# Two sets of small products taken over the whole TensorE array, and the written-out order of a layer made from other costs and waits

## The chip, the core and the metric

The kernel runs on one core of one Trainium2 chip. The metric is the device time of one execution in microseconds (us), from the first to the last instruction with what lies around them. A core has a matrix engine (TensorE, PE in the profile, with its weight loads as PEld), a vector engine (VectorE, DVE), a scalar engine (ScalarE, ACT), GpSimd (POOL) and SyncE (SP), which here only issues loads. Each engine works off its own list of instructions in the order in which the program wrote them; an instruction that waits for another engine holds up everything behind it in its own list.

## The reference

One layer of a hybrid decoder is computed for 256 tokens of a new sequence and for 8 running sequences ("samples") of 8 tokens each, 320 tokens in all. All arithmetic is float32:

```python
h = rms_norm(x, norm_g)
p = einsum('nld,dp->nlp', h, w_in)              # 2048 -> 12416 columns
# branch A, 16 heads of 64: RWKV-7 state, one step per token
sa = einsum('nhvk,nhk->nhv', s, kk_t)
s  = s * w_t - sa (kk_t * a_t)^T + v_t k_t^T;   y_t = s r_t
# branch B, 8 heads of 128: gated linear recurrence
S_t = diag(g_t) S_{t-1} + k_t v_t^T;            o_t = S_t^T q_t
merged = sigmoid(ga) * (y_a @ proj_a) + sigmoid(gb) * (y_b @ proj_b)
y = rms_norm(x + merged @ w_out, final_norm_g)
```

The states after the last token of every sequence are outputs too; the samples start from states that are loaded.

## The kernel before

**Stages.** A start stage normalizes and transposes x. Then comes the long stage this text is about, here the *recorded stage*: 64 column tiles of `w_in` that the heads need, and four gate tiles, each multiplied with the 320 tokens, and in between them all the recurrence work of eight head groups (one group is two heads of branch A and one head of branch B). After it the remaining gate tiles, `proj_a`, `proj_b` and `w_out` follow.

**Stream.** Float32 weights and activations are each split into a rounded high part and a remainder, and a product is three matmuls: high by high, high by low, low by high. A column tile is 16 times three matmuls of 128x128 weights with 320 columns into the tile `mps`. The text calls these matmuls the *stream*. The weights come in blocks of 512 KB (`raw`, by SyncE), ScalarE copies the high part (`whi`), VectorE subtracts for the remainder (`wlo`); each has three buffers.

**Head work.** `rwkv` (L706) and `hgrn` (L1071) hold the recurrences in a form for matmuls. For branch B a 64-token chunk is worked by levels: `level` (L1118) makes scaled keys and queries `kq` for block sizes 8 to 128, `products` (L1139) multiplies them, and `keep` (L1145) copies the wanted triangles of the result out of PSUM (`b`) into `att` by a mask. `products` runs one matmul for each 64-token chunk: 64 columns of weights, 64 columns streamed, and neighbouring chunks go to the upper and the lower half of the PSUM partitions, so that two such matmuls use two halves of the array's columns. In branch A `samples` (L980) multiplies the samples' states `s0t` with `arz` in the same way, eight matmuls for a group. These float32 matmuls are not split by the program; the profile shows each of them as two passes (two records).

**Order.** The recorded stage isn't issued as it is written. `Recorder` (L69) takes every call down as an `Op` with a cost in ns by engine and shape (`add`), finds who must wait for whom (`link`, L141), and then plays the engines against the clock (`order`, L175). At each step `choose` (L191) takes the engine that can begin first and picks an operation on it: on PE a small matmul in the whole-array shape as soon as it is ready, small matmuls of other shapes (`part`) together, those of `hgrn` after a wait of up to 6000 ns (`WAIT`), and else the next matmul of the stream; on VectorE and ScalarE the weight splits first when the stream comes within 4500 ns of them, else what has the longest chain behind it. A small matmul on whose result an operation depends counts as late by `LAT` and by a margin of 250 ns (`MARGIN`). The result is one fixed list for each engine (L1340); on the chip, semaphores keep the data right, and a list that was made from wrong times shows as waits.

**What the costs know.** In the plan of before each engine runs by itself: VectorE's and GpSimd's operations never delay each other. A load that overwrites a buffer which a store still reads (the state `s0`, loaded at L718 and L1073 and stored at the end of the group before, all issued by GpSimd) may in the plan follow that store at once.

Of the kernel before, what the change touches and what calls it, by code (L numbers as in the profile page):

```python
# [12 lines left out]
AF = mybir.ActivationFunctionType  # L13
# [35 lines left out]
class Op:  # L49
    __slots__ = ("eng", "fn", "args", "kw", "cost", "lat", "uses", "mode", "passes", "cols", "stream",  # L50
                 "succ", "npred", "ready", "rank", "block", "margin", "wait", "n")
# [17 lines left out]
class Recorder:  # L69
    APART, MARGIN, WAIT = 10, 250, 6000  # L70
# [14 lines left out]
    def add(self, eng, name, fn, args, kw):  # L85
        o = Op()
        o.eng, o.fn, o.args, o.kw, o.n = eng, fn, args, kw, len(self.ops)
        aps = [x for x in (*args, *kw.values()) if hasattr(x, "start_partition")]
        out = aps[0]
        free = 1  # L90
        for d in out.shape[1:]:
            free *= d
        o.uses = []
        for j, x in enumerate(aps):
            t_ = x.tensor
            if "DRam" in type(t_).__name__:
# [5 lines left out]
        o.lat = self.LAT[eng]  # L102
        o.mode = None
# [71 lines left out]
    def order(self):  # L175
# [8 lines left out]
        mode, done, left = (128, 128), [], len(self.ops)  # L184
        bigs = [o for o in self.ops if o.eng == "PE" and o.stream]
# [5 lines left out]
        def choose(e):  # L191
# [3 lines left out]
            t_ = max(now, min(o.ready for o in q))  # L195
# [17 lines left out]
            can = [o for o in q if o.ready <= t_ + 30]  # L213
# [8 lines left out]
        while left:  # L222
            t_, o = min((choose(e) for e in ready if ready[e]), key=lambda x: x[0])
# [5 lines left out]
            if o.eng == "PE":  # L229
# [5 lines left out]
                if o.stream:  # L235
                    gone += 1
            free[o.eng] = end = start + cost
# [9 lines left out]
def hybrid_step(ctx, tc, x_prompt, x_sample, state_rwkv, state_hgrn, state_shift, norm_g, w_in,  # L247
# [384 lines left out]
    def ring(pool, tag, shape, bufs, dt, size, clear=False):  # L632
# [12 lines left out]
        if len(shape) == 2:  # L645
# [5 lines left out]
             "w1": 320, "w2": 320, "w3": 320, "ks": 128, "ket": 256}  # L651


    CLEAR = {"uB", "uE", "ys", "rhs", "rhs2", "k3", "vm"}
# [51 lines left out]
    def rwkv(p, r, k, vp, za):  # L706
# [273 lines left out]
        def samples():  # L980
            ps = aps("psr")
            for sp in range(4):
                for h in range(2):
                    T.matmul(ps[HS[h], 32 * sp:32 * sp + 32], s0t[:, sp, 64 * h:64 * h + 64],
                             arz[:, sp, :, h].rearrange("p b x i -> p b (x i)"), start=True, stop=True)

            sr0, sr1 = at("sr0", (128, 2, 64)), at("sr1", (128, 64))
            p4 = ps[:, :128].rearrange("p (s x i) -> p x s i", x=2, i=8)
            V.tensor_copy(sr0.rearrange("p h (s i) -> p h s i", i=8), p4[:, 0:1].to_broadcast([128, 2, 8, 8]))
            S.copy(sr1.rearrange("p (s i) -> p s i", i=8), p4[:, 1])  # L990
# [80 lines left out]
    def hgrn(hd, q, k, v, zb):  # L1071
# [37 lines left out]
        k0 = bt("k0", tag="w1")  # L1109
        S.activation(k0, x, AF.Exp, scale=-1.0)  # L1110
        V.tensor_mul(q0, q0, q)
        V.tensor_mul(k0, k0, k)
# [5 lines left out]
        def level(sz, tag):  # L1118
            half = lambda t_: t_[:, :NP_].rearrange("p (b two s) -> p b two s", two=2, s=sz)
            kq = bt("kq", (128, NP_), tag=tag)  # L1120
            if sz == 32:
# [23 lines left out]
        def keep(ps, o_, n):  # L1145
            for c_ in range(2):
                sl = HS[c_]
                V.copy_predicated(att[sl, :NP_].rearrange("p (j c t) -> p j c t", c=2, t=64)[:, :, c_],
                                  mu8[sl, None, n].to_broadcast([64, 2, 64]),
                                  ps[sl, o_:o_ + 128].rearrange("p (j t) -> p j t", t=64))  # L1150
# [3 lines left out]
        products(ps, 0, k0, q0, 5)  # L1154
        products(ps, 256, kq8, kq8)
        keep(ps, 0, 0)
        V.copy_predicated(att[0:64, NP_:], mu8[0:64, 0], ps[0:64, 128:192])
# [19 lines left out]
        ps = bps("pke")  # L1177
        T.transpose(ps[0:64, :128], es[:, 1], ident)
        k3 = bt("k3", (128, 2, 128), dt=F32R)
# [8 lines left out]
        T.matmul(ps[:, 256:320], vt[0:64, 2], att[0:64, NP_:], start=True, stop=True)  # L1188
# [18 lines left out]
        for j in range(2):  # L1207
            T.matmul(ps[HS[j], 128:192], kq32[:, 64 * j:64 * j + 64], kq32[:, 128 + 64 * j:192 + 64 * j],
                     start=True, stop=True)
        for j in range(2):  # L1210
            T.matmul(ps[HS[j], 192:256], kq64[:, 128 * j:128 * j + 64], kq64[:, 128 * j + 64:128 * j + 128],
                     start=True, stop=True)
        keep(ps, 0, 2)
        for j in range(2):
            for b in range(2):
                V.tensor_copy(att[64 * b:64 * b + 32, 128 * j + 64 * b + 32:128 * j + 64 * b + 64],
                              ps[64 * j + 32 * b:64 * j + 32 * b + 32, 128 + 32 * b:160 + 32 * b])
            V.tensor_copy(att[0:64, 128 * j + 64:128 * j + 128], ps[HS[j], 192:256])
# [289 lines left out]
```

## Time and profile before

| what | value |
|---|---|
| median of 3 runs | 1195.76 us (1194.38 to 1198.14) |
| profiled execution, its own time | 1195.58 us |
| its span, first to last instruction | 1193.8 us |
| busy, share of the span: PE, PEld, DVE, ACT, POOL | 96%, 92%, 66%, 56%, 22% |
| the chain that ended last: PE, DVE, ACT | 82%, 8%, 3% |
| recorded stage, first to last stream matmul of its list (L1341) | 35.4 to 755.5 us |

A line of the profile names the source line, the engine, the operation, the tile written and the tiles read (`out<-in`), shapes and counts. All operations of the recorded stage have one line, L1341, and many tiles share a ring: `a` is any PSUM tile of `rwkv`, `b` any of `hgrn`, `w` the rings w1 to w3 of `hgrn` (levels, keys, queries), `s` the states. "Idle before" is the time in which the engine did nothing, with what ended it. PE's matmuls overlap in the pipeline, so a matmul's duration is longer than its distance to the next one; costs on PE are read here as distances between starts.

### The profile page before, as it was taken

To read this page: it belongs to the slowest core of one execution; us is meant where nothing else is said; L and a number is where in the kernel's file an instruction comes from. 1 tells how busy PE (TensorE), PEld (TensorE's weight loads), DVE (VectorE), ACT (ScalarE), POOL (GpSimd) and SP (SyncE) were. 2 spreads that over 40 slices of the span, in tenths; PEclk is the share of its full clock that TensorE was granted. 3 is DMA by queue.
4 is the path that set the end of the run, shared out by engine and by line. 5 is a ranking of instruction groups with operands and counts; after the bars stand their busy time and mean duration, and the time that the engine had idled before them with its cause. 6 is when DMAs were issued, how large, how long until landed. Compare 5 with 4: busy or idle time off the path is not lost.

```text
span 1193.8 us, 21136 instructions
## 1 busy us (share of the span) xinstructions
PE 1151.3 (96%) x7976; PEld 1096.4 (92%) x7976; DVE 790.3 (66%) x1618; ACT 666.3 (56%) x1463; POOL 258.5 (22%) x493
## 2 busy tenths in 40 slices
PE   5999999999999999999998999999999999999997
PEld 4898998998998998999998998999999999998875
DVE  7678878778868968869777877644344444435552
ACT  6566765766666667557666666544444444434431
POOL 7642333243323323413413312000000000000000
PEclk9899999999999999999999999999999999999999
DMA  6442543543534534524534435555555555575542
GB/s 181 127 136 81 160 121 89 148 122 91 148 106 128 144 85 113 146 80 127 139 110 113 131 83 137 151 150 151 146 155 147 154 145 156 144 254 163 169 135 88
DMA packets 251424, 159.72 MB, mean 134 GB/s; under 512 B 5609, under 2 KB 237338, under 8 KB 250682
## 3 DMA queue, kind: packets, MB, share of 16 engines
q1 hardware_dynamic: 246106, 140.68, 41.3%
q0 software_dynamic: 5216, 17.68, 5.4%
q8 instruction: 63, 1.03, 0.4%
q14 instruction: 39, 0.32, 0.1%
HBM read 148.53 MB, written 9.81 MB: 133 GB/s over the span
## 4 chain that ended last, share of the span: by engine, by line
PE 82%; DVE 8%; ACT 3%; DMA 2%; POOL 2%; issue 2%; DVEq 0%; SPq 0%; ACTq 0%; POOLq 0%
PE mps L1341 36%; PE a L1341 10%; PE mps L313 6%; PE mps L312 6%; PE mps L311 6%; PE b L1341 3%; DMA raw<-in_w_out_dram 2%; PE po L1423 2%; PE po L1421 2%; PE po L1422 2%; PE ppb L313 2%; PE ppa L313 2%; PE ppb L312 2%; PE ppa L312 2%; PE ppb L311 2%
## 5 line engine op out<-in xcount | busy, mean ns | idle before, releaser
L1341 PE MATMUL mps<-hlo,whi 128*128 128x320 f32 x1088 | 347.1, 319 | 0.0
L1341 PE MATMUL mps<-hhi,wlo 128*128 128x320 f32 x1088 | 346.4, 318 | 0.4 <-DVE wlo L1341 0.4
L1341 PE MATMUL mps<-hhi,whi 128*128 128x320 f32 x1088 | 344.7, 317 | 1.9 <-ACT whi L1341 1.9
L1341 PEld LDWEIGHTS mps<-hhi,whi 128*128 128x128 f32 x1088 | 206.3, 190 | 3.7 <-ACT whi L1341 2.2
L1341 PEld LDWEIGHTS mps<-hhi,wlo 128*128 128x128 f32 x1088 | 206.4, 190 | 2.4 <-DVE wlo L1341 0.8
L1341 PEld LDWEIGHTS mps<-hlo,whi 128*128 128x128 f32 x1088 | 206.5, 190 | 1.2 <-issue 0.6
L302 DVE TENSOR_TENSOR wlo<-raw,whi 128x1024 fp32r<-128x1024 f32 x88 | 107.7, 1225 | 125.0 <-ACT whi L301 124.8
L1341 DVE TENSOR_TENSOR wlo<-raw,whi 128x1024 fp32r<-128x1024 f32 x134 | 168.9, 1261 | 20.2 <-ACT whi L1341 19.0
L301 ACT CAST whi<-raw 128x1024 fp32r<-128x1024 f32 x88 | 92.1, 1048 | 161.1 <-PE mps L312 107.2
L1341 ACT CAST whi<-raw 128x1024 fp32r<-128x1024 f32 x134 | 140.3, 1048 | 73.5 <-PE mps L1341 70.6
L311 PE MATMUL mps<-hhi,whi 128*128 128x320 f32 x464 | 145.0, 312 | 0.0
L312 PE MATMUL mps<-hlo,whi 128*128 128x320 f32 x464 | 144.7, 312 | 0.0
L313 PE MATMUL mps<-hhi,wlo 128*128 128x320 f32 x464 | 144.7, 312 | 0.0
L313 PEld LDWEIGHTS mps<-hhi,wlo 128*128 128x128 f32 x464 | 88.3, 190 | 0.0
L312 PEld LDWEIGHTS mps<-hlo,whi 128*128 128x128 f32 x464 | 88.2, 190 | 0.0
L311 PEld LDWEIGHTS mps<-hhi,whi 128*128 128x128 f32 x464 | 88.1, 190 | 0.0
L1414 DVE TENSOR_TENSOR wlo<-raw,whi 128x1024 fp32r<-128x1024 f32 x32 | 39.0, 1224 | 44.5 <-ACT whi L1413 44.4
L1396 POOL DMA_DIRECT2D xb<-in_x_sample_dram x1 | 0.5, 546 | 312.9 <-PE mps L313 312.9
L1413 ACT CAST whi<-raw 128x1024 fp32r<-128x1024 f32 x32 | 33.5, 1050 | 54.3 <-PE po L1426 23.3
L1423 PE MATMUL po<-wlo,mhi 128*128 128x512 f32 x128 | 50.4, 394 | 0.9 <-DVE wlo L1414 0.9
L1421 PE MATMUL po<-whi,mhi 128*128 128x512 f32 x128 | 50.2, 392 | 0.7 <-DVE gbt L1381 0.7
L1422 PE MATMUL po<-whi,mlo 128*128 128x512 f32 x128 | 50.0, 391 | 0.0
(418 smaller groups left out, 2356.0 us busy)
## 6 DMA issues: line engine op xcount, KB each, us to landing
raw<-in_w_in_dram SPq DMA_DIRECT2D x194, 512.0 KB
raw<-in_w_out_dram SPq DMA_DIRECT2D x32, 512.0 KB
raw<-in_proj_a_dram SPq DMA_DIRECT2D x16, 512.0 KB
raw<-in_proj_b_dram SPq DMA_DIRECT2D x16, 512.0 KB
s<-in_state_hgrn_dram POOLq DMA_DIRECT2D x8, 512.0 KB, 5.5
out_dram<-s POOLq DMA_DIRECT2D x8, 512.0 KB, 4.6
s<-in_state_rwkv_dram POOLq DMA_DIRECT2D x8, 256.0 KB, 4.0
out_dram<-s POOLq DMA_DIRECT2D x8, 256.0 KB, 3.3
```

Of the source, the lines that this page charges most:

```text
L301: S.copy(hi[:, ks], raw[:, ks])
L302: sub.tensor_sub(lo[:, ks], raw[:, ks], hi[:, ks].bitcast(F32))
L311: T.matmul(dst, hi[:, q, :], xhi[:, k, :], start=(k == 0), stop=False)
L312: T.matmul(dst, hi[:, q, :], xlo[:, k, :], start=False, stop=False)
L313: T.matmul(dst, lo[:, q, :], xhi[:, k, :], start=False, stop=(k == nk - 1))
L1341: o.fn(*o.args, **o.kw)
L1396: G.dma_start(yx[j], src)
L1413: S.copy(hi, raw)
L1414: V.tensor_sub(lo, raw, hi.bitcast(F32))
L1421: T.matmul(pt, h, hi, start=first, stop=False)
L1422: T.matmul(pt, l, hi, start=False, stop=False)
L1423: T.matmul(pt, h, lo, start=False, stop=end)
```

## The change

On TensorE: `products` multiplies 128 tokens with 128 tokens in one matmul over the whole array and `keep` picks the two 64-token diagonal blocks out of the larger result; levels 32 and 64 become one matmul each; the samples' part of the first level gets a matmul of its own, later, beside the transposition of `es`; the samples' `vt` by `att` runs over all 128 rows, with the unused rows cleared once; the state products become four matmuls in place of eight, and `sr0` and `sr1` are copied out in two halves each.

In the plan: every operation has a mark `port` if it needs the port that VectorE and GpSimd are taken to share, and `hold` if it keeps the other engine from it (two inputs that are not in PSUM, or a VectorE copy or `tensor_scalar` all in SBUF). An operation with `port` begins no earlier than the other engine's hold ends, less 130 ns. A load waits in the plan for the landing of a store that reads its buffer (4500 ns). The fixed costs of VectorE, ScalarE and GpSimd operations are changed.

The core of the diff (the bookkeeping around it, and shapes that only follow, are left out):

```diff
+        two = sum("PSUM" not in str(x.space) for x in aps[1:] if tuple(x.shape[1:]) != (1,)) > 1
+        o.hold = two and eng in "VG"
+        o.port = two and eng == "V" or eng == "G" and "dma" not in name
...
-            o.cost = (free / 2 if two else free) / 0.96 + (215 if two else 157)
+            o.cost = (free / 2 if two else free) / 0.96 + (150 if two else 157)
+            if two:
+                o.hold = o.port = True
+            if any(tuple(x.shape[1:]) == (1,) and free > 1 for x in aps[1:]):
+                o.cost += 55
...
-            o.cost = 190 + free / 1.2
+            o.cost = (150 if name == "copy" else 200) + free / 1.2
+            if name == "copy" and not o.uses[1][5]:
+                o.cost += 40
...
-            o.cost = 950 if "dma" in name else 250 + free * (0.35 if name == "memset" else 1.75)
+            o.cost = 950 if "dma" in name else 95 + free * 0.88 if name == "memset" else 200 + free * 1.66
...
-                            pred.setdefault(u[3].n, (u[3], psum and u[3].eng != "PE"))
+                            pred.setdefault(u[3].n, (u[3], psum and u[3].eng != "PE" or u[3].dma))
...
+            if e in port:
+                held = port["G" if e == "V" else "V"] - self.OVER
+                if e == "V" and held > now and port["G"] == free["G"]:
+
+                    held += min((o.cost for o in ready["G"] if o.hold and o.ready <= free["G"] - 40), default=0.0)
+                at_ = {o: max(now, o.ready, held if o.port else 0.0) for o in q}
+                t_ = min(at_.values())
...
-            for h in range(2):
-                    T.matmul(ps[HS[h], 32 * sp:32 * sp + 32], s0t[:, sp, 64 * h:64 * h + 64],
-                             arz[:, sp, :, h].rearrange("p b x i -> p b (x i)"), start=True, stop=True)
+                T.matmul(ps[:, 64 * sp:64 * sp + 64], s0t[:, sp], arz[:, sp].rearrange("p b h x i -> p (b h x i)"),
+                         start=True, stop=True)
...
-        def products(ps, o_, kq, q_, n=4):
-            for c_ in range(n):
-                tk_ = slice(64 * c_, 64 * c_ + 64)
-                T.matmul(ps[HS[c_ % 2], o_ + 64 * (c_ // 2):o_ + 64 * (c_ // 2) + 64], kq[:, tk_], q_[:, tk_],
-                         start=True, stop=True)
+        def products(ps, o_, kq, q_):
+            for j in range(2):
+                tk_ = slice(128 * j, 128 * j + 128)
+                T.matmul(ps[:, o_ + 128 * j:o_ + 128 * j + 128], kq[:, tk_], q_[:, tk_], start=True, stop=True)
...
-        products(ps, 0, k0, q0, 5)
+        products(ps, 0, k0, q0)
...
         ps = bps("pke")
+        T.matmul(ps[:, 128:192], k0[:, NP_:], q0[:, NP_:], start=True, stop=True)
...
-        T.matmul(ps[:, 256:320], vt[0:64, 2], att[0:64, NP_:], start=True, stop=True)
+        T.matmul(ps[:, 256:320], vt[:, 2], att[:, NP_:], start=True, stop=True)
...
-        for j in range(2):
-            T.matmul(ps[HS[j], 128:192], kq32[:, 64 * j:64 * j + 64], kq32[:, 128 + 64 * j:192 + 64 * j],
-                     start=True, stop=True)
-        for j in range(2):
-            T.matmul(ps[HS[j], 192:256], kq64[:, 128 * j:128 * j + 64], kq64[:, 128 * j + 64:128 * j + 128],
-                     start=True, stop=True)
+        T.matmul(ps[:, 256:384], kq32[:, 0:128], kq32[:, 128:256], start=True, stop=True)
+        T.matmul(ps[:, 384:512], kq64[:, 0:128], kq64[:, 128:256], start=True, stop=True)
```

More of the change, by code (lines that the diff above doesn't have):

```diff
@@ L50 @@
     __slots__ = ("eng", "fn", "args", "kw", "cost", "lat", "uses", "mode", "passes", "cols", "stream",
-                 "succ", "npred", "ready", "rank", "block", "margin", "wait", "n")
+                 "succ", "npred", "ready", "rank", "block", "margin", "wait", "port", "hold", "dma", "n")
 def span_of(ap):
@@ L102, in add @@
         o.lat = self.LAT[eng]
+        o.dma = "dma" in name
         o.mode = None
@@ L130, in add @@
         elif eng == "S":
-            o.cost = 190 + free / 1.2
+            o.cost = (150 if name == "copy" else 200) + free / 1.2
+            if name == "copy" and not o.uses[1][5]:
+                o.cost += 40
+            if any(tuple(x.shape[1:]) == (1,) and free > 1 for x in aps[1:]):
+                o.cost += 60
         elif eng == "G":
-            o.cost = 950 if "dma" in name else 250 + free * (0.35 if name == "memset" else 1.75)
+            o.cost = 950 if "dma" in name else 95 + free * 0.88 if name == "memset" else 200 + free * 1.66
             if "dma" in name:
@@ L184, in order @@
         mode, done, left = (128, 128), [], len(self.ops)
+        port = {"V": 0.0, "G": 0.0}
         bigs = [o for o in self.ops if o.eng == "PE" and o.stream]
@@ L194, in choose @@
             now = free[e]
-            t_ = max(now, min(o.ready for o in q))
+            if e in port:
[4 more added lines that the diff above has]
+                t_ = min(at_.values())
+            else:
+                t_ = max(now, min(o.ready for o in q))
             if e == "PE":
@@ L212, in choose @@
                 return max(t_, o.ready), o
-            can = [o for o in q if o.ready <= t_ + 30]
+            can = [o for o in q if (at_[o] if e in port else o.ready) <= t_ + 30]
             def worth(o):
@@ L222, in order @@
         while left:
-            t_, o = min((choose(e) for e in ready if ready[e]), key=lambda x: x[0])
+            t_, o = min((choose(e) for e in ready if ready[e]), key=lambda x: (x[0], x[1].eng == "V"))
             ready[o.eng].remove(o)
@@ L236, in order @@
                     gone += 1
+            if o.port:
+                start = max(start, port["G" if o.eng == "V" else "V"] - self.OVER)
+            if o.hold:
+                port[o.eng] = start + cost
             free[o.eng] = end = start + cost
@@ L982, in samples @@
             for sp in range(4):
-                for h in range(2):
-                    T.matmul(ps[HS[h], 32 * sp:32 * sp + 32], s0t[:, sp, 64 * h:64 * h + 64],
-                             arz[:, sp, :, h].rearrange("p b x i -> p b (x i)"), start=True, stop=True)
+                T.matmul(ps[:, 64 * sp:64 * sp + 64], s0t[:, sp], arz[:, sp].rearrange("p b h x i -> p (b h x i)"),
+                         start=True, stop=True)
             sr0, sr1 = at("sr0", (128, 2, 64)), at("sr1", (128, 64))
-            p4 = ps[:, :128].rearrange("p (s x i) -> p x s i", x=2, i=8)
-            V.tensor_copy(sr0.rearrange("p h (s i) -> p h s i", i=8), p4[:, 0:1].to_broadcast([128, 2, 8, 8]))
-            S.copy(sr1.rearrange("p (s i) -> p s i", i=8), p4[:, 1])
+            for h in range(2):
+                p4 = ps[HS[h], :256].rearrange("p (s h x i) -> p h x s i", h=2, x=2, i=8)[:, h]
+                V.tensor_copy(sr0[HS[h]].rearrange("p h (s i) -> p h s i", i=8),
+                              p4[:, 0:1].to_broadcast([64, 2, 8, 8]))
+                S.copy(sr1[HS[h]].rearrange("p (s i) -> p s i", i=8), p4[:, 1])
             yield
```

27 lines of the change are left out of this document (14 added, 13 removed).

## The prediction

> **What bounds the kernel now.** I read the page first, then two stretches side by side, then the longest piece of the chain that ended last.
>
> ```profile
> span 1193.8 us, 21136 instructions
> ```
> ```profile
> L1341 PE MATMUL mps<-hhi,whi 128*128 128x320 f32 x1088 | 344.7, 317 | 1.9 <-ACT whi L1341 1.9
> ```
> ```profile
> 35.30:755.50 720.20, 700.64 (x5246) 671.16 (x5245) 570.40 (x1352) 463.90 (x1155) 230.69 (x428) 0.99 0.43 119
> 755.50:1000.00 244.50, 244.50 (x1669) 244.50 (x1669) 110.04 (x134) 110.21 (x164) 0.00 (x0) 1.00 0.54 153
> ```
> ```profile
> 743.46 12.02 PE mps L1341 x82
> ```
>
> The columns of the two stretches are length, busy time with count for PE, PEld, DVE, ACT and POOL, granted clock, DMA share and GB/s. TensorE bounds everything. Behind 755.5 it is never idle, and nothing of the change runs there, so what the recorded stage gains or loses, the end gains or loses in full. In the stage the stream takes 12.02/82 = 0.147 us for each matmul. There are three groups of 1088 like the one quoted, 3264 in all, so 478 us of the 720.2 are stream. The other 242 are small matmuls and waits. PE is idle for 720.20 - 700.64 = 19.6 us. The stage's last small matmul ends before 743.46, and 12 us of pure stream follow, so a longer chain of head work at the end is covered by that much.
>
> Who ends PE's waits, with us in total, times and the longest:
>
> ```profile
> PE b L1341 <- DVE att L1341: 4.0, 5, 1.1
> PE a L1341 <- POOL uB L1341: 2.5, 3, 1.1
> PE a L1341 <- DVE st L1341: 2.3, 2, 1.8
> PE b L1341 <- POOL vm L1341: 2.0, 2, 1.6
> ```
>
> These four are 10.8 us in 12 waits; the rest of the 19.6 is scattered. At the same rate there are some 22 waits. A stream matmul is drawn as lasting 0.317 us (quoted above) though the next could start after 0.147, so each wait loses about 0.17 more than its idle time: 19.6 + 22 x 0.17 makes 23 us lost to waits. That is all that a better order can win.
>
> **Part 1: the matmuls over the whole array.** The costs, as distances between starts on PE, first for whole-array passes:
>
> ```profile
> 202.24 0.31 PE L1341 MATMUL mps<-hhi,wlo 128*128 128x320 f32 x1
> 202.38 0.38 PE L1341 MATMUL a<-st,arp 128*128 128x128 f32 x2
> 202.60 0.39 PE L1341 MATMUL y<-arp,st 128*128 128x128 f32 x2
> 202.74 0.39 PE L1341 MATMUL mps<-hhi,whi 128*128 128x320 f32 x1
> 202.97 0.31 PE L1341 MATMUL mps<-hlo,whi 128*128 128x320 f32 x1
> ```
>
> From 202.24 to 202.97 are 0.73 us with two stream matmuls (0.294) in it: 0.436 for four passes, 0.109 a pass. The new products are of that shape or half as many columns, which I price the same. Now the old ones: the late levels with the samples' `att` product, the state products, and the early levels.
>
> ```profile
> 204.60 0.31 PE L1341 MATMUL mps<-hhi,whi 128*128 128x320 f32 x1
> 204.84 0.43 PE L1341 MATMUL b<-att,vt 64*128 64x64 f32 x2
> 205.20 0.69 PE L1341 MATMUL b<-w 128*64 128x64 f32 x16
> 205.82 0.41 PE L1341 MATMUL mps<-hlo,whi 128*128 128x320 f32 x1
> 206.07 0.40 PE L1341 MATMUL b<-vm,k 128*128 128x512 f32 x1
> ```
> ```profile
> 271.95 0.31 PE L1341 MATMUL mps<-hlo,whi 128*128 128x320 f32 x1
> 272.19 0.66 PE L1341 MATMUL a<-arz,s0t 128*64 128x32 f32 x16
> 272.78 0.41 PE L1341 MATMUL mps<-hhi,wlo 128*128 128x320 f32 x1
> 273.03 0.38 PE L1341 MATMUL a<-rhs,yz 128*128 128x128 f32 x2
> ```
> ```profile
> 363.10 0.50 PE L1341 MATMUL b<-w,w 128*64 128x64 f32 x9
> ...
> 363.67 0.59 PE L1341 MATMUL a<-s0t,uv 128*64 128x512 f32 x1
> ```
>
> The late levels and `att` cost 1.47 - 0.294 = 1.18 us. New they are two matmuls for level 16, one each for 32 and 64 and one for `att`, ten passes, 1.09: a gain of 0.09. The state products cost 1.08 - 0.294 = 0.79. New they are four matmuls, eight passes, 0.87: a loss of 0.08. The early levels are 18 passes (nine in the first row, nine in the rows left out) from 363.10 until the next kind starts at 363.67, 0.57. New they are ten passes, 1.09: a loss of 0.52, because half-array passes go in pairs, 0.032 each, and whole ones do not pair.
>
> A group loses 0.51, eight groups 4.1 us. All of it lies on PE, the engine that sets the end, with no cover. Upper bound: the early levels shared their change of array shape with neighbours of the same shape, which may now stand alone. Sixteen state passes at 0.032 are 0.51 of 0.79, so a change costs (0.79 - 0.51)/2 = 0.14; two more for each group add 2.2, to 6.3. Lower bound: the stream matmul at 202.97 comes 0.23 after the one before it, 0.08 more than 0.147; if neighbours hide this step in all three places of the eight groups, 1.9 less, which leaves 2.2. I take 4.1, by the rows of the same shape.
>
> The copies that follow cost PE nothing: `sr0` is two VectorE copies instead of one of this kind,
>
> ```profile
> 185.93 0.29 DVE L1341 COPY sr<-a 128x128 f32<-128x128 f32 x1
> ```
>
> so 0.29 more on the samples' chain of each group (a like step on ScalarE), under the stream, which has work at that time. Without that cover it would be 8 x 0.29 = 2.3 us. The number of masked copies is unchanged, and the clearing of `w1` and `vt` is once.
>
> **Part 2: the order.** What a wrong plan looks like:
>
> ```profile
> 81.09 1.39 DVE L1341 TENSOR_TENSOR wlo<-raw,whi 128x1024 fp32r<-128x1024 f32 x1
> ...
> 81.34 1.33 POOL L1341 COPY uB<-id 128x160 f32<-128x160 f32 x1
> ```
> ```profile
> L1341 POOL COPY uB<-id x8: 328/435/1328, 81.3 to 680.7; 128x160 f32<-128x160 f32 x8
> ```
> ```profile
> 631.37 2.92 DVE L1341 TENSOR_TENSOR wlo<-raw,whi 128x1024 fp32r<-128x1024 f32 x1
> ```
>
> The GpSimd copy takes 0.435 by the median (minimum, median, maximum in ns) and 1.33 when `wlo` is running; its three waits of 2.5 us on PE are this. `wlo` itself takes 2.92 at 631.37 in place of 1.39 or less, with a GpSimd product running, and PE's wait of 1.8 for `st`, which is next on VectorE, follows from that. The plan of before knows none of it; the new one does. The second blind spot is a load behind a store:
>
> ```profile
> POOL s L1341 <- DMA out_dram<-s: 36.8, 11, 4.7
> ```
> ```profile
> 625.98 0.89 POOL L1341 DMA_DIRECT2D s<-in_state_rwkv_dram  x1 [3.72 <-DMA out_dram<-s]
> ...
> 626.88 1.05 POOL L1341 TENSOR_TENSOR vm<-v,seq 96x512 fp32r<-96x512 f32 x1
> ```
>
> GpSimd stood 3.72 us before this load, `vm` was queued behind it, and PE's longest wait for `vm` (1.6) followed. With the load put where the store has landed, the GpSimd operations behind it come earlier; the load itself comes no later than it does now, since it waits for the same landing.
>
> How much goes? Of the four rows (10.8 us) I take three quarters, since I can follow most of `uB`, `st` and `vm` to these two causes but only part of `att`; of the other 8.8 half. That is 12.5 of 19.6 idle, and with 23/19.6 for the full loss 14.7 us. New waits come in: the level products used to be held back up to 6 us until they went together, so their operands were there; now each goes when the plan thinks it ready. Small passes number 5246 - 3264 = 1982, and 23 us over them is 0.012 each; 28 new passes for each of eight groups, 224, bring 2.6 at today's error and half of it, 1.3, at a smaller one. Net gain 13.4. Bounds: none of it, or all but 2 us of 23.
>
> A rule speaks for a blind spot in the new model: it lets a GpSimd operation hold the port only if it has two inputs, so a GpSimd copy holds up nothing. Here is a copy, a two-input VectorE subtraction that starts 0.04 into it, and the whole group of such subtractions:
>
> ```profile
> 227.53 0.21 POOL L1341 COPY shc<-pad 128x9 f32<-128x9 f32 x1 [1.78 <-ACT pad L1341]
> ...
> 227.57 0.51 DVE L1341 TENSOR_TENSOR dif<-pad 128x328 f32<-128x328 f32 x1 [1.38 <-ACT pad L1341]
> ```
> ```profile
> L1341 DVE TENSOR_TENSOR dif<-pad x24: 474/500/511, 47.4 to 665.7; 128x328 f32<-128x328 f32 x24
> ```
>
> A block would have held the subtraction for the copy's remaining 0.17; it took 0.51, and all 24 took 0.474 to 0.511. The Trainium skill (SBUF — State Buffer, "Who interferes with whom") says that a VectorE instruction with two SBUF inputs contends with any GpSimd instruction that reads SBUF, and a copy reads it; by that rule the sum would be the one of the second rival. The trace speaks against it in this row.
>
> **The sum.** 1195.58 (profiled, against a median of 1195.76, so 0.18 is added) + 4.1 - 13.4 + 0.18 = 1186.5 us.
>
> **The rivals.** *Nearly all waits go.* The new costs fit the engines, and 21 of 23 us are saved: 1195.8 + 4.1 - 21 = 1179. For it: the port and the stores stand behind the longest waits. Against it: nearly half of the idle time is scattered over causes that I did not follow.
>
> *The copies block too, or the list is only shuffled.* The model misses GpSimd's copies, waits of about half the size stay, and the gain is 6.7: 1195.8 + 4.1 - 6.7 = 1193.2. Row 227.53 speaks against the blocking. That the order does not become better at all gives 1199.9, the upper end of this case.
>
> *Slower: the products lose their cover.* With no gain by the order, the 4.1 to 6.3 of part 1 stay, and the 224 passes that go as soon as the plan allows bring 2.6 of new waits: 1195.8 + 6.7 to 8.9, about 1203.5. The place is the level products of each head, waiting on VectorE's `w`. It decides from the point at which the better order saves less than about 3 us of waits. For it: whole passes cost three times the half ones in the early levels. Against it: it needs the port model to do nothing.
>
> **Chances.** About 0.3% of 1195.8, 3.6 us, is what a measurement of this kernel can tell from no change. Forecast case (1182 to 1192) 0.50; nearly all waits go 0.20; half of them stay, or the list is only shuffled 0.19, of it 0.04 for copies that block; lost cover 0.11. Faster by over 3.6 us, below 1192.2: the first two and a little of the third, 0.72. Within: 0.17. Slower: 0.11. The range 1178 to 1198 leaves out the lost cover, the far end of the third case, and a little beyond 1178.
>
> **What would show it.** Part 1 is right if the early levels are whole-array passes at 0.11 and the state products eight passes for 0.87. Part 2 is right if PE's idle time between 35 and the end of the stage falls from 19.6 to near 8, no `uB` copy takes over 1 us, and GpSimd's wait for `out_dram<-s` (36.8) nearly vanishes. Wrong: PE waiting on `w` before level products, idle time unchanged, or a stage whose small matmuls cost less than before.

## The result, and the profile after

The changed kernel takes 1184.95 us (median of 4 runs, 1184.38 to 1187.72) against 1196.38 of the kernel before on the same chip (4 runs, 1194.38 to 1198.14): a ratio of 0.991, 95% interval 0.9887 to 0.9932. The profiled execution took 1184.47. Its page, the two stretches (columns as in the prediction) and, in an excerpt, the waits of PE:

```profile
span 1182.8 us, 20773 instructions
```
```profile
34.60:743.60 709.00, 693.45 (x5051) 677.28 (x5050) 568.15 (x1362) 464.52 (x1163) 233.16 (x430) 1.00 0.45 122
```
```profile
755.50:1000.00 244.50, 244.50 (x1669) 244.50 (x1668) 109.43 (x134) 107.64 (x161) 0.00 (x0) 1.00 0.53 150
```
```profile
PE a L1365 <- DVE wst L1365: 5.4, 1, 5.4
PE a L1365 <- DVE uv L1365: 4.0, 2, 3.4
PE a L1365 <- ACT uv L1365: 3.9, 1, 3.9
PE a L1365 <- ACT rh L1365: 1.3, 1, 1.3
PE a L1365 <- DVE pp L1365: 0.6, 1, 0.6
PE mps L1365 <- DVE wlo L1365: 0.4, 1, 0.4
```

The span is 11.0 us shorter, and the recorded stage 10.8 (from first to last stream matmul 719.8 before, 709.0 now); the end is as it was, with PE never idle. PE's idle time in the stage fell only from 19.6 to 15.6, but its form is another: the scattered waits of before are gone, and three long ones make up 12.7 of what is left. Two signs that the prediction named, in the groups and among GpSimd's waits:

```profile
L1365 POOL COPY uB<-id x8: 325/427/485, 83.9 to 669.1; 128x160 f32<-128x160 f32 x8
```
```profile
POOL s L1365 <- DMA out_dram<-s: 11.0, 8, 3.4
```

No `uB` copy takes over 0.485 us (1.328 before), and GpSimd waits 11.0 us for stores (36.8). The new matmuls, on the timeline of PE:

```profile
186.48 0.31 PE L1365 MATMUL mps<-hhi,wlo 128*128 128x320 f32 x1
186.63 1.00 PE L1365 MATMUL a<-arz,s0t 128*128 128x64 f32 x8
187.44 0.39 PE L1365 MATMUL mps<-hhi,whi 128*128 128x320 f32 x1
187.67 0.61 PE L1365 MATMUL b<-w,w 128*128 128x128 f32 x4
188.03 0.39 PE L1365 MATMUL mps<-hlo,whi 128*128 128x320 f32 x1
188.26 0.31 PE L1365 MATMUL mps<-hhi,wlo 128*128 128x320 f32 x1
```

From 187.44 to 188.03 are 0.59 us with one stream matmul (0.147) in it: 0.443 for four passes, 0.111 each. The state products take 187.44 - 186.63 = 0.81 for eight passes.

**An account of the stage.** Idle time leaves out what a short wait costs when the pipeline still shows a matmul as running. So I also took the distances between starts on PE: the stage's length, less 3263 stream steps of 0.1469 us (479.3), less the whole-array passes at their measured distances (165.3 us with the old matmuls, 190.0 with the new), less the half-array matmuls and the changes of the array's shape at the median of each kind (36.9 with the old, 18.0 with the new). What remains is *lost to waits*: before 719.8 - 479.3 - 165.3 - 36.9 = 38, after 709.0 - 479.3 - 190.0 - 18.0 = 22. Two kernels with the same matmuls compare without it, by the length of the stage alone. Between the old and the new matmuls it is an estimate that hangs on the prices. If each distance is priced by all distances between matmuls of the same shapes in the traces of ten of the kernels below, the new matmuls cost from 1 us less to 4 us more than the old ones, as one takes the median or the lowest tenth for the price; by the account above they cost 5.8 more.

**What a long wait costs behind itself.** The granted clock around the wait of 3.9 us, which ended at 534.03 (columns as in the prediction, the clock is the third from the end):

```profile
531.48:534.89 3.41, 0.86 (x8) 0.86 (x8) 2.73 (x5) 1.38 (x6) 1.51 (x2) 1.00 0.09 20
534.89:538.30 3.41, 3.41 (x17) 3.41 (x16) 1.88 (x8) 1.60 (x6) 0.00 (x0) 0.50 0.00 0
538.30:541.71 3.41, 3.41 (x25) 3.30 (x25) 2.97 (x6) 1.32 (x4) 2.64 (x4) 1.00 0.01 1
```

For 3.41 us behind the wait the clock was granted at half, and a stream step there takes 0.267 us in place of 0.147 (stream matmuls start at 537.07, 537.33 and 537.60). That loses 3.41 x (1 - 0.147/0.267) = 1.5 us, in which PE counts as busy. Not every long wait has such a stretch behind it: the one of 3.4 us has none. In the profiled executions the stage has 10.2 us at half clock before and 6.8 after. This loss is in "lost to waits", and PE's idle time leaves it out.

### The profile page after: what moved, and what is told of

The parts are those of the page before. It is cut to its first block, busy times and chain, and to the rows that moved or that the text cites. A ratio compares the mean times of both kernels' runs of the same rounds, so it can differ in the third digit from the quotient of the medians.

```text
span 1182.8 us, 20773 instructions
## 1 busy us (share of the span) xinstructions
PE 1144.1 (97%) x7784; PEld 1102.4 (93%) x7784; DVE 785.5 (66%) x1626; ACT 666.0 (56%) x1471; POOL 260.9 (22%) x495
## 4 chain that ended last, share of the span: by engine, by line
PE 88%; DVE 5%; DMA 3%; ACT 3%; POOL 1%; issue 1%; DVEq 0%; SPq 0%; ACTq 0%; POOLq 0%
PE mps L1365 38%; PE a L1365 12%; PE mps L338 6%; PE mps L339 6%; PE mps L337 6%; PE b L1365 4%; DMA raw<-in_w_out_dram 2%; PE po L1447 2%; PE po L1445 2%; PE po L1446 2%; PE ppb L338 2%; PE ppa L338 2%; PE ppb L339 2%; PE ppa L339 2%; PE ppb L337 2%; PE ppa L337 2%
```

## The experiments

"Ratio" is against the kernel before on the same chip. The last two columns are of the profiled execution, whose time lies up to 3.2 us from the median (no port below it, plan starts late above it).

| kernel | median, us | ratio [95%] | stage, us | lost to waits, us |
|---|---|---|---|---|
| before, beside after | 1196.38 | | 719.8 | 38 |
| after | 1184.95 | 0.991 [0.9887, 0.9932] | 709.0 | 22 |
| matmuls only | 1192.55 | 0.9979 [0.9963, 0.9994] | 719.0 | 32 |
| plan only | 1185.04 | 0.9906 [0.9888, 0.9923] | 709.9 | 28 |
| no port | 1198.42 | 1.0021 [1.0008, 1.0034] | 722.7 | 35 |
| no wait for stores | 1186.48 | 0.9922 [0.9907, 0.9936] | 710.1 | 23 |
| plan only, not held back | 1195.07 | 0.9988 [0.9975, 1.0] | 719.9 | 38 |
| plan starts late | 1186.0 | 0.9916 [0.989, 0.9942] | 713.7 | 26 |
| issue holds the port | 1183.74 | 0.9899 [0.9874, 0.9924] | 707.0 | 20 |
| both of these | 1177.63 | 0.9858 [0.9838, 0.9879] | 700.1 | 13 |
| whole products held back | 1185.59 | 0.9915 [0.9903, 0.9928] | see there | see there |

**The two parts, each alone.** The first kernel has the new matmuls and the whole old `Recorder`, the second the new `Recorder` and the old matmuls:

```diff
-        o.hold = two and eng in "VG"
...
-            if e in port:
...
                 T.matmul(ps[:, o_ + 128 * j:o_ + 128 * j + 128], kq[:, tk_], q_[:, tk_], start=True, stop=True)
```


> The whole-array products alone, ordered by the plan of before. Theory A (the account on record): the products cost TensorE 4.1 us more (2.2 to 6.3) and the waits stay as they are or grow a little by lost cover, so 1198 to 1204 us, against about 1196 for before. Theory B (the early levels were dearer than they looked between their neighbours, so the products cost nothing or less than nothing): 1192 to 1197.


```diff
         o.hold = two and eng in "VG"
...
-                T.matmul(ps[:, o_ + 128 * j:o_ + 128 * j + 128], kq[:, tk_], q_[:, tk_], start=True, stop=True)
+                T.matmul(ps[HS[c_ % 2], o_ + 64 * (c_ // 2):o_ + 64 * (c_ // 2) + 64], kq[:, tk_], q_[:, tk_],
+                         start=True, stop=True)
```


> The new plan alone, with the half-array products of before. Theory A: the order brings some 15 us and the products took 4 back, so this is faster than the changed kernel: 1179 to 1183 us. Theory B: the order brings what the whole change brings, 1184 to 1188. If the new plan only helps because whole-array products need no grouping: above 1189.

The plan alone gives all of it: 1185.04, so the products did not take 4 us back. With the same matmuls on both sides it shortens the stage by 9.9 us (719.8 to 709.9) and by 10.0 (719.0 to 709.0). The matmuls alone are not slower but slightly faster, 1192.55 against 1195.44, 0.9979, with an interval that ends below 1; beside the new plan they change nothing (1185.04 and 1184.95). Why they are not slower is open. In the account they cost PE 24.7 us in new passes and take away 18.9 of old ones, 5.8 more, and since the stage is 0.8 shorter, the time lost to waits would fall by 6.5 us, with the old plan (38 to 32) as with the new one (28 to 22). By the other prices they cost from 1 us less to 4 more, and the waits fall by 5 us at most or not at all. PE's idle time in the stage went from 19.6 to 18.0 with the old plan and from 15.4 to 15.6 with the new one. So the second theory of the first run, that the products cost nothing, stands beside the account: its range, 1192 to 1197, held.

**The parts of the plan.** The first kernel keeps the new costs and the wait for stores, but no operation has `port` or `hold`; the second only forgets the stores:

```diff
+        o.port = o.hold = False
...
-                o.hold = o.port = True
+                pass
```


> The changed kernel with the port taken out of the plan; costs and the wait of loads for stores stay. Theory A: the port is the main cause of the saved waits, so most of the gain is gone: 1191 to 1198 us, and long VectorE subtractions beside GpSimd products stand again before TensorE's waits. Rival: the corrected costs or the stores carry the gain: 1183 to 1188.


```diff
-                            pred.setdefault(u[3].n, (u[3], psum and u[3].eng != "PE" or u[3].dma))
+                            pred.setdefault(u[3].n, (u[3], psum and u[3].eng != "PE"))
```


> The changed kernel with the plan letting a load follow the store of its buffer at once. Theory A: GpSimd stands before loads again for some 35 us in all, and 1 to 4 us of waits return to TensorE: 1186 to 1189. Rival: the loads were hidden anyway and nothing changes: 1184 to 1186.

Without the port the kernel is slower than before, 1198.42. The group of `uB` copies shows what came back, with the two waits of PE for it:

```profile
L1366 POOL COPY uB<-id x8: 322/434/1395, 82.6 to 679.4; 128x160 f32<-128x160 f32 x8
```
```profile
PE a L1366 <- POOL uB L1366: 2.5, 2, 1.3
```

So the new costs and the rule for stores bring nothing on their own here: the kernel with the same matmuls and the whole old plan took 1192.55. Taking the port out loses the plan's whole gain; whether the port would bring it with the old costs was not run. What the port changes shows on VectorE, too: in the stage, its operations that take over 0.3 us longer than the lower quartile of their kind number 40 before, 41 with the matmuls only and 38 without the port, but 30 with the plan only and 23 after. Without the rule for stores GpSimd stands longer for them than before the change, and the time hardly moves (1.5 us, intervals that overlap): little if any of those waits of GpSimd was PE's.

```profile
POOL s L1365 <- DMA out_dram<-s: 47.4, 12, 6.2
```

**If the whole-array products save waits, why?** Two candidates: they go at once, where the old ones were held back up to 6 us, or they spare changes of the array's shape. First the plan alone, with nothing held back:

```diff
-    APART, MARGIN, WAIT, OVER = 10, 250, 6000, 130
+    APART, MARGIN, WAIT, OVER = 10, 250, 0, 130
```


> The new plan with the half-array products (as in the run of the plan alone, 1185.0 us), but branch B's half-array matmuls are no longer held back for up to 6000 ns until they can go together. Theory C: holding the products back is what cost waits, because everything behind them came late and close together, and whole-array products freed about 6.5 us of waits by going at once; then this one loses some waits too and pays for more changes of array shape instead: 1180 to 1186. Theory D: what counts is that products in the shape of the stream need no change of array shape; then more changes make it slower: 1187 to 1192.

With half-array products, going at once costs 10 us (1185.04 to 1195.07), more than either theory had allowed. Counted on PE, the shape changes from 106 to 137 times; 31 changes at the prediction's 0.14 are 4.3 us, so less than half of the loss; the rest lies in waits that I have not followed. Then the reverse, the changed kernel with its whole-array products held back:

```diff
+                if not any(o.late and t_ - o.ready >= o.wait for o in own):
+                    own = [o for o in own if not o.late]
...
-                    pool = [o for o in can if o.stream]
+                    pool = [o for o in can if o.stream] or can
...
-        T.matmul(ps[:, 256:384], kq32[:, 0:128], kq32[:, 128:256], start=True, stop=True)
+        T.matmul(ps[:, 256:384], kq32[:, 0:128], kq32[:, 128:256], start=True, stop=True).late = True
```


> The changed kernel, but the level products of branch B, though whole-array, wait in the plan until one of them has been ready for 6 us, as they did before the change; the rest of the costs and matmuls are those of after. Theory H (the whole-array products save waits because they need no change of the array's shape): nothing much is lost, 1184 to 1187, ratio about 0.991. Theory I (they save waits because they go at once and so what depends on them comes earlier): the 6.5 us come back in part or whole, 1187 to 1192, ratio 0.993 to 0.997.

The total is that of after, 1185.59, but made of two halves. The stretch up to its last stream matmul, and from there to 760:

```profile
35.40:733.40 698.00, 690.41 (x5027) 673.44 (x5026) 560.60 (x1339) 454.29 (x1141) 229.49 (x426) 1.00 0.45 123
733.40:760.00 26.60, 22.98 (x128) 20.86 (x127) 14.27 (x26) 16.23 (x32) 2.23 (x4) 0.87 0.38 106
```

The stream is through at 733.4, 10 us earlier than in after, and only then come the last two dozen small matmuls: the head work has become too late for the stream to cover, PE is idle for 3.6 us, and the clock is granted at 0.87. Going at once is therefore not what shortens the stage up to its last stream matmul; it is what lets the head work end under the stream. That the fewer shape changes (103 before, 64 with the new matmuls in the old plan, 61 in after) offset the price of the new passes fits both kernels, but no run shows it by itself.

**The three long waits left.** The first, 5.4 us, is at the start of the stage:

```profile
43.08 0.60 POOL L1306 CAST lora_a<-lora_a 64x320 fp32r<-64x320 f32 x1
43.74 0.20 POOL L1365 COPY pad<-sst 128x8 f32<-128x8 f32 x1
43.91 0.73 POOL L1365 DMA_DIRECT2D w2a<-in_rwkv_w_dram  x1
...
46.18 0.30 ACT L1365 CAST wst<-w2a 64x128 fp32r<-64x128 f32 x1 [3.51 <-DMA w2a<-in_rwkv_w_dram]
46.51 0.28 DVE L1365 TENSOR_TENSOR wst<-w2a,wst 64x128 fp32r<-64x128 f32 x1 [3.14 <-ACT wst L1365]
...
46.94 0.60 PE L1365 MATMUL a<-lora_w,wst 128*128 128x320 f32 x1 [5.39 <-DVE wst L1365]
```

PE begins the stage at 34.6, and the plan takes every engine to be free then. GpSimd is busy with the start stage (line L1306) until 43.7, issues the load of `w2a` at 43.9, and PE reaches the matmul that needs it long before. The other two look like this one:

```profile
446.93 0.97 POOL L1365 DMA_DIRECT2D out_dram<-s  x1 [2.92 <-DVE s L1365]
447.01 0.31 ACT L1365 ACTIVATE w<-R 128x128 f32<-128x128 f32 x1 [0.33 <-DVE R L1365]
447.01 0.29 DVE L1365 TENSOR_TENSOR F<-F 128x128 f32<-128x128 f32 x1
...
447.22 3.77 DVE L1365 TENSOR_TENSOR w<-w,f 128x128 f32<-128x128 f32 x1
...
447.93 1.91 POOL L1365 TENSOR_TENSOR s<-s,dec 128x1024 f32<-128x1024 f32 x1
449.78 1.04 POOL L1365 TENSOR_TENSOR vm<-v,seq 96x512 fp32r<-96x512 f32 x1
```

VectorE's `w`, otherwise 0.28 us, begins 0.7 before the product `s` and ends when the product behind that one, `vm`, is through; `uv`, for which PE waits, is next on VectorE. What lies beside its beginning is only the issue of a store, and the plan lets an issue hold nothing. I tried to see such an issue by itself, with work added behind the outputs of the changed kernel:

```diff
+                V.tensor_add(mt_["mu"], mt_["ml"][:, :64], pts[0][:, :64])
+                G.dma_start(mt_["ml"], x_prompt[0, 0:128, 0:256])
+                if case in ("product", "psum"):
+                    G.tensor_mul(mt_["mo"], mt_["mx"], mt_["mx"])
...
+                V.tensor_copy(mt_["mc"], pts[0][:, :128])
+                V.tensor_add(mt_["mb"], mt_["mx"][:, :64], pts[0][:, :64] if case == "psum" else mt_["mx"][:, 64:128])
```


> The changed kernel with a measurement behind its last output, so its time is longer and not compared: VectorE does a two-input subtraction-like addition of 64 columns (some 0.2 us) while GpSimd issues a load; behind the load GpSimd has a two-input product, nothing, a copy, a memset, or a product with VectorE's second input in PSUM, four times each. Theory E: a product that is queued behind the load's issue takes the port already, so VectorE waits through the issue and the product in the first case alone: over 1 us there, 0.2 us in the other four. Rival: issuing a load or a store holds the port by itself: long in the first four cases, short with PSUM. Second rival: the two long waits of the changed kernel were something else: 0.2 us everywhere.

This told nothing, in its one execution: in every case VectorE's addition (0.21 to 0.22 us) began 0.18 us before GpSimd's issue or earlier, and was over as the issue began. The second attempt lets VectorE run 14 additions of 128 columns back to back, so that one of them always meets the issue (one execution, each case four times):

```diff
+                V.tensor_add(mt_["mu"], mt_["ml"][:, :64], mt_["mo"][:, :64])
+                if "load" in case:
+                    G.dma_start(mt_["ml"], x_prompt[0, 0:128, 0:128])
+                if "product" in case:
+                    G.tensor_mul(mt_["mo"], mt_["mx"], mt_["mx"])
+                elif "copy" in case:
+                    G.tensor_copy(mt_["mo"], mt_["mx"])
+                for j in range(14):
+                    V.tensor_add(mt_["mb"], mt_["mx"][:, :128], mt_["mx"][:, 128:256])
```


> Adds work of its own behind the outputs of the changed kernel: GpSimd issues a load and/or does a 512-column product (or copy) while VectorE runs 14 two-input additions of 128 columns back to back (0.28 us each alone); its total time is not compared. Theory E (an issue keeps VectorE's two-input operations out once it is under way, if a two-input product is queued directly behind it): with load+product one addition that starts inside the issue, a few tenths of a us or more before the product begins, lasts until the product ends, 1.3 us and more; with the product alone an addition is held for about the product, 1.05 us plus what it had left, and starts at most 0.3 us before the product does; with the load alone and with load+copy all additions last 0.28 to 0.35. Theory F (the issue itself does nothing, and the two long VectorE operations in the trace had another cause): with load+product no addition starts more than 0.3 us before the product and lasts into it; it looks like the product alone. Theory G (any issue takes the port): additions of 0.6 us and more beside the load alone too.

One repetition of load and product, one of load and copy, and one of the load alone, on the timeline (the issue, then what the engines did around it):

```profile
775.43 0.54 POOL L1516 DMA_DIRECT2D ml<-in_x_prompt_dram  x1 [6.47 <-DVE mb L1522]
```
```profile
775.70 1.50 DVE L1522 TENSOR_TENSOR mb<-mx 128x128 f32<-128x128 f32 x1
776.00 1.05 POOL L1518 TENSOR_TENSOR mo<-mx 128x512 f32<-128x512 f32 x1
```
```profile
767.81 0.54 POOL L1516 DMA_DIRECT2D ml<-in_x_prompt_dram  x1 [7.15 <-DVE mb L1522]
768.34 0.62 POOL L1520 COPY mo<-mx 128x512 f32<-128x512 f32 x1
```
```profile
768.07 1.05 DVE L1522 TENSOR_TENSOR mb<-mx 128x128 f32<-128x128 f32 x1
```
```profile
792.27 0.29 DVE L1522 TENSOR_TENSOR mb<-mx 128x128 f32<-128x128 f32 x1
```

The last row started 0.27 us into an issue with nothing behind it and was not held. In front of a product, the addition at the same point lasted 1.50, to the product's end; so it was in two of four repetitions (1.50 both times), while in the other two the held addition began with the product or after it (1.13, 1.22). With the product alone the held addition always began 0.16 to 0.29 us after it. By the bound that I had set (more than 0.3 us before the product; 0.29 came out both times) the product's case doesn't part the first two theories. What parts them is that with the product alone no held addition began before it, that `w` in the stage began 0.7 before, and the copy: it held an addition that began 0.27 before it for 1.05 us in all four repetitions. So the issue alone holds nothing (the third theory falls), and an issue with work behind it holds VectorE from within the issue on; but on the copy the first theory was wrong too. That raised a new question: does a copy take the port by itself?

```diff
+                elif "memset" in case:
+                    G.memset(mt_["mo"], 0.0)
```


> Adds work of its own behind the outputs, as the kernel with VectorE's additions beside a load's issue did; its total time is not compared. GpSimd now does a copy or a memset of 512 columns, alone and directly behind the issue of a load, beside the same run of 14 additions. There the copy behind an issue held one addition for 1.05 us each time, although the recorded stage shows two-input operations untouched beside copies. Theory J (a copy takes the port as a product does, with or without an issue): beside the copy alone one addition of 0.6 us and more in each of the four repetitions. Theory K (only a copy that stands directly behind an issue does): beside the copy alone all additions last 0.28 to 0.35, and those beside load+copy 1.05 again. The memset reads nothing and should hold nothing alone; if any operation directly behind an issue holds, load+memset shows an addition of 0.7 us and more.

A copy without an issue before it, and a memset behind an issue:

```profile
775.99 0.61 POOL L1520 COPY mo<-mx 128x512 f32<-128x512 f32 x1 [5.56 <-DVE mu L1514]
776.16 0.58 DVE L1524 TENSOR_TENSOR mb<-mx 128x128 f32<-128x128 f32 x1
```
```profile
800.21 0.29 DVE L1524 TENSOR_TENSOR mb<-mx 128x128 f32<-128x128 f32 x1
```

It does: in three of four repetitions one addition took 0.58 to 0.59 us, twice its time, to the copy's end. In the first the copy was the one that waited (1.54 us), behind a weight subtraction `wlo` that had begun 0.15 before it; the addition after that took 0.70, to the copy's end. Behind an issue, the copy held one addition for 1.04 in three repetitions again; in the first, two took 0.58. The expectation had put 0.6 as the mark, so the size is a little under it, but the other theory's 0.28 to 0.35 is excluded. The memset held nothing, with or without an issue (the second row is an addition beside it).

**Better plans.** Two lines follow: the plan's clock for GpSimd, VectorE and ScalarE begins when the start stage lets them go, and an issue holds the port. Each alone:

```diff
         free = dict.fromkeys(self.real, 0.0)
+        free["G"], free["V"], free["S"] = 9100.0, 8500.0, 8000.0
```


> The changed kernel, but the plan lets GpSimd, VectorE and ScalarE begin 9.1, 8.5 and 8.0 us after the stream, as the trace shows them to be busy with the start stage until then. Theory F: the wait of 5.4 us for the first weights of the decay goes and nothing takes its place: 1178 to 1181. Rival: the first head group is late anyway and PE waits for something else of it: 1184 to 1187.


```diff
-        o.hold = two and eng in "VG"
+        o.hold = two and eng in "VG" or eng == "G" and "dma" in name
```


> The changed kernel, but in the plan GpSimd's issue of a load or store keeps VectorE's two-input operations away too. Theory E: the two waits of 3.4 and 3.9 us, where VectorE stood through an issue and two products, go: 1177 to 1181. Rival: the longer holds make the plan wrong elsewhere and new waits come: 1184 to 1188.

With the late start alone, the wait of 5.4 went, but the time did not fall, as the rival had it: the two waits behind issues stayed (3.4 and 3.9), and a new list brought new ones (2.4 for `whi`, 1.8 for `ket`). Its stage of 713.7 is from the slowest of its four executions (1189.16), with 20.5 us at half clock. With the issue holding the port the two waits went, but as in its rival new ones came, three for `ket` with 5.4 us in all, and the wait at the start became 5.8 us for `whi`: 1183.74, within the intervals the same as after. Both together, with the two diffs above:

> The changed kernel with both additions to the plan: GpSimd's DMA issues hold the port, and GpSimd, VectorE and ScalarE are taken to be busy until 9.1, 8.5 and 8.0 us of the plan. If the two add up, the start wait of 5.4 us and the two waits of 3.4 and 3.9 behind the issues are all gone, and 1184.9 becomes about 1178 to 1180. If each new list brings scattered waits of its own, as in the run with the late start alone (about 6 us of the big waits came back elsewhere), it comes out at 1182 to 1186.

```profile
35.40:735.50 700.10, 691.74 (x5051) 675.85 (x5050) 569.55 (x1362) 464.27 (x1163) 238.86 (x430) 1.00 0.44 123
```
```profile
PE b L1366 <- ACT ket L1366: 5.4, 3, 1.8
```

1177.63 us, below both kernels; its interval (0.9838 to 0.9879) lies under that of after. All three long waits are gone. Each of these plans is one list, so how much of the 7.3 us is the two facts and how much a lucky list is not shown. PE's idle time in the stage is 8.4, with 3.4 us at half clock, and 5.4 of it is one pattern, three times: a VectorE operation that begins as one GpSimd product ends is held through the next, which follows directly, with no issue between.

```profile
109.24 1.05 POOL L1366 TENSOR_TENSOR vm<-v,seq 96x512 fp32r<-96x512 f32 x1 [2.97 <-PE mps L1366]
110.14 2.15 DVE L1366 TENSOR_TENSOR F<-F 128x128 f32<-128x128 f32 x1
110.25 1.89 POOL L1366 TENSOR_TENSOR s<-s,dec 128x1024 f32<-128x1024 f32 x1
```

## Why the prediction was right, point by point

The forecast was 1186.5; 1184.95 was measured. The sum, -9.3 us, is near the stage's -10.8, but that is in part luck, since two of its steps failed and made up for each other: the matmuls with their new waits were to cost 5.4 us and, alone, saved 2.9, and the order was to save 14.7 and saved 10. What held is the cause: the plan that knows the port.

- *Whole-array passes at 0.109, state products 0.87, 4.1 us in all.* The price of a pass held (0.111). The state products took 0.81. The exchange as a whole is not settled: 5.8 in the account, inside the range of 2.2 to 6.3, but from 1 us less to 4 us more by the other prices. So it is open, too, whether the small matmuls came out cheaper than before, which the prediction had named as a sign of being wrong.
- *"New waits come in", 1.3 us, since products are no longer held back.* Failed: with the matmuls alone PE's idle time in the stage fell from 19.6 to 18.0, and the kernel is no slower. That waits went away, 6.5 us by the account, is not shown. The rival in which the products lose their cover stood on the same thought, and the kernel with the matmuls alone refutes it where it had put the danger: no wait over 0.3 us stands before a level product.
- *14.7 us saved by the order.* Too much: with either set of matmuls the new plan takes some 10 us off the stage, as above.
- *"19.6 + 22 x 0.17 makes 23 us lost to waits. That is all that a better order can win."* Failed: from the kernel with the matmuls only to the one with both additions, whose matmuls are the same, the order has won 18.9 us of the stage (719.0 to 700.1), and 8.4 of idle time are left there, which makes 27. PE shows matmuls as running through short waits, and 22 waits with 0.17 each covered too few of these. The half clock behind long waits, some 4.6 us of the stage before (10.2 x (1 - 0.147/0.267)), stood in no term.
- *Two blind spots, the port and the loads behind stores.* The first held, and the gain hangs on it: without it 1198.42. The second was real on GpSimd and worth little or nothing to PE: 47.4 us of such waits and 1186.48.
- *The signs.* The `uB` copies and GpSimd's wait for stores came as named, though the wait fell to 11.0, not to nearly nothing. "From 19.6 to near 8" failed: 15.6, since three long waits took the place of the scattered ones. The start of the stage and the issue that holds the port stood in no row that I had read.
- *The rule that speaks against the model.* The prediction set row 227.53 against it, a copy of 9 columns, 0.21 us long. The row did not show what a larger copy does; why it showed no block is open. The Trainium skill (SBUF — State Buffer, "Who interferes with whom") says that a VectorE instruction with two SBUF inputs contends with a GpSimd instruction that reads SBUF and not with one that only writes; the copy and the memset of 512 columns agree with it, 0.58 against 0.29 us. The step's end, that little hangs on it here, held all the same: with small copies (`uB`, 160 columns, is among the longest) the model without them gained its 10 us.

## What to carry to other kernels

When an order is written out from a model, a list that fits better can leave a few long waits in place of many short ones, as here. Follow each of them to the engine that stood still, since it can name a fact that the model lacks, and try the facts together as well as singly: here each alone gained nothing clear, and both gained 7.3 us. Size what an order can win from the distances between starts on the bounding engine, not from its idle time, and look at the granted clock behind each long wait. Run a change of shape on that engine by itself: its passes, priced one by one, said 4.1 us slower, and the kernel was 2.9 faster.

## What the runs showed of the hardware

- GpSimd's issue of a load or store, with nothing or a memset behind it, held no VectorE addition (0.29 us). With a product or a copy directly behind it, an addition that began about 0.27 us into an issue of 0.54 was held to the end of that work: 1.50 and 1.05 us. In the stage, with two products behind the issue, 3.77. With no issue between two products, an operation that began 0.15 us before the end of the first was held to the end of the second, 2.15.
- A GpSimd copy of 512 columns (0.61 us) held one addition for 0.58; a memset (0.53 us) none. Where a subtraction of 1024 columns (1.22 us) had begun 0.15 before the copy, the copy waited instead and took 1.54. The Trainium skill (the same section) says that issue order decides which of the two blocks; the copy's 1.54 agrees.
- The clock fell to half for stretches of 3.41 us, with stream steps of 0.267 in place of 0.147. No single long gap is needed for it: in the kernel with products held back such stretches began at 747.75 and 754.58, each right behind 3.41 us in which PE was idle for 1.6 and 1.8 us in gaps of at most 0.99. As much idle time did not always bring one: in after, 1.73 us idle from 449.56 to 452.97 did not.
